# Delta-net stage of a two-layer trunk: background modulation held back during the block inverses, its weights in other buffers, longer planned inverse steps

## The chip, the cores and the metric

The kernel runs on one core of one Trainium2 chip. The metric is the device time of one execution in microseconds (us), as the median of several runs. One execution was also recorded by the hardware profiler; durations and starts below come from that one.

A core has five engines that run side by side, each with an instruction queue of its own that is worked off in order: TensorE (PE in the profile; PEld is its weight load), VectorE (DVE), ScalarE (ACT), GpSimd (POOL) and SyncE (SP), which here only starts transfers. A `q` behind an engine's name is its sequencer, which issues DMAs and waits on semaphores.

## The reference

A trunk of two layers on x of shape 1024 x 1024 (float32). Each layer is a mixer, a layer norm, a convolutional feed-forward and a layer norm; layer 0 mixes with a gated delta net, layer 1 with retention. Every layer is modulated by a condition vector:

```
e = silu(c @ cond_w + cond_b)
for i in range(2):
    mod = e @ ada_w[i] + ada_b[i]
    sh1, sc1, g1, sh2, sc2, g2 = split(mod, 6)
    y = mixers[i](x * (1 + sc1) + sh1)
    x = layer_norm(alpha * x + (1 + g1) * y)
    y = conv_ffn(x * (1 + sc2) + sh2)
    x = layer_norm(alpha * x + (1 + g2) * y)
```

The delta net, which the change touches, has 8 heads of width 128 and chunks of 64 positions:

```
q, k, v = split(silu(causal_dwconv((h @ w_in)[qkv])))
kk  = strict_lower(kb @ k.T * decay)
sol = triangular_solve(kk + eye, [v * beta, kb * exp(gc)])      # u, w
scan over chunks:  v_new = u - w @ state
                   o = (q * exp(g)) @ state + qk @ v_new
                   state = state * exp(g_last) + (k * exp(g_last - g)).T @ v_new
o = rmsnorm(o) * norm_w * silu(z);  return o @ w_out
```

The vectors of `mod` that later steps of layer 0 need (sc2, sh2, g1) are computed inside the delta-net stage, as "background modulation".

## The kernel before, in words

**Filler.** The big matmuls of the stage are those of `h @ w_in`: a unit makes 128 output features for all 1024 positions, as two halves of 8 x 3 matmuls of 128x128 by 128x512 (each product is made of three, because the operands are split into a high and a low part). There are three leftover halves ("h"), 21 units for q, k and v ("c" items) and eight gate units ("z" items). `filler` (L1028 to L1071) runs them in the order of `items` (L1080); a "c" item takes two of the 24 `qkv` buffers, and when fewer than two are free and more than four gate units are left, a gate unit is taken in its place (L1032). A unit's weights come by one 512 KB transfer into the two-buffer tag `wr` (L102), are split by ACT (L89) and DVE (L90, `wl`), and each half of a "c" unit costs DVE three convolution steps (L435).

**Background modulation.** `bg_ada` queues eight units for each of three vectors (24 in all, L1017 to L1019). A unit loads 256 rows of `ada_w` (512 KB, tile `mvw`, L210), in the tag `bg_tag[0]`, which is `wr` here, and DVE adds the two 128-row blocks, weighted by `e`, onto the one `ada` tile (L214, L216). Every fourth unit is followed by four transposes on PE (L226) and four ACT sums (L228). `filler` calls `bg_step` once after every "c" and "z" item (L1071).

**Block inverse.** The triangular solve goes by an explicit inverse. `t_solve` (L766) inverts the 32x32 diagonal blocks of four heads at once, on DVE: `X` is gathered by ACT (L773), transposed (L777), and then 31 steps of a multiply (L785) and a subtract (L787) run one after the other; at every second step the function yields `LAT["fs"]` (L788). Then come a transpose (L791), a copy on ACT (L793) and another transpose (L795). There are two such solves, for heads 0 to 3 and 4 to 7.

**The rest of the heads' work.** `t_front` makes the matrices U (L719 to L764), `t_chain` joins the 32-blocks to 64-blocks with small matmuls on PE (L807 to L888), `prep` and `dt_half` make scaled v, k and q-k products (L897, L898, L932, L933, with `DT` loaded at L925 into a `lane` or `auh` buffer), and `scan` runs the 8 chunk steps of each head (L940), with a `tail` per half head (L988).

**What sets the order.** `run` (L627) is a planner in the Python that builds the program: it keeps a clock `clk` that every PE instruction advances by a planned cost (0.216 us for a 512-wide matmul), and of the streams whose time has come it always goes on with the one of the lowest priority number; a stream that yields a number sleeps for that much planned time. The filler has priority 9.0, a solve 0.3 and 2.3. PE's order is fixed by this plan (`pq`, L607). The other engines' orders are not pinned: the framework orders each of them from the instructions' dependencies and a timeline of its own, in which an instruction that comes later in the program can go ahead when it is ready; buffers of a tag are handed out in program order.

Of the kernel before, what the change touches and what calls it, by code (L numbers as in the profile page):

```python
# [12 lines left out]
ALU = mybir.AluOpType  # L13
AX = mybir.AxisListType

P = 128
D = 1024
S = 1024
KT = D // P
HALF = 512  # L20
# [13 lines left out]
def trunk_kernel(ctx: ExitStack, tc, A):  # L34
    nc = tc.nc
    pe, act, dve, pool, sp = nc.tensor, nc.scalar, nc.vector, nc.gpsimd, nc.sync
# [9 lines left out]
    def tl(tag, shape, dt=F32, name=None):  # L46
        return sb.tile(shape, dt, tag=tag, name=name or tag, bufs=BUFS[tag])
# [66 lines left out]
    bg = []  # L114

    bg_ps = [None]
    bg_tag = ["wr"]

    def bg_step(tile=mm_tile):
        bg_ps[0] = tile  # L120
        if bg:
            bg.pop(0)()
# [58 lines left out]
    e = ct("e", [P, KT])  # L181
# [19 lines left out]
    def bg_ada(i, j, kind):  # L201
        box = {}

        def unit(nh, kp):
            if kp == 0:
                box["a"] = tl("ada", [P, HALF])
            a = box["a"]
            wr = tl(bg_tag[0], [P, 2, HALF], name="mvw")
            c0 = j * D + nh * HALF
            sp.dma_start(wr, A["ada_w"][i, kp * 256:(kp + 1) * 256, c0:c0 + HALF].rearrange("(a p) n -> p a n", p=P))  # L210
            for kk in range(2):
                k = kp * 2 + kk
                if k == 0:
                    dve.tensor_scalar(a, wr[:, 0], e[:, 0:1], None, ALU.mult)  # L214
                else:
                    dve.scalar_tensor_tensor(a, wr[:, kk], e[:, k:k + 1], a, ALU.mult, ALU.add)  # L216
            if kp < KT // 2 - 1:
                return
            if kind == "col":
                if nh == 0:  # L220
                    vecs[i, j] = ct(f"v{i}{j}", [P, KT])
                gs = slice(4 * nh, 4 * nh + 4)
                v, b = vecs[i, j][:, gs], bias_cols(i, j)[:, gs]
                tp, pt = bg_ps[0](), tl("sm2", [P, 4], name="cs")
                for g in range(4):
                    pe.transpose(tp[:, g * P:(g + 1) * P], a[:, g * P:(g + 1) * P], ident)  # L226
                for g in range(4):
                    act.activation(a[:, g * P:(g + 1) * P], tp[:, g * P:(g + 1) * P], AF.Copy, accum_out=pt[:, g:g + 1])  # L228
                if j in (1, 2, 4):
                    dve.scalar_tensor_tensor(v, pt, 1.0, b, ALU.add, ALU.add)  # L230
                else:
                    dve.tensor_add(v, pt, b)
            else:
                if nh == 0:
                    rows[i, j] = row_load(A["ada_b"][i:i + 1, j * D:(j + 1) * D], ("x", i))
                g = rows[i, j][nh]
                pt = bg_ps[0]()
                pe.matmul(pt, ones, a, start=True, stop=True)
                dve.scalar_tensor_tensor(g, pt, 1.0, g, ALU.add, ALU.add)

        for nh in range(2):
            for kp in range(KT // 2):
                bg.append(lambda nh=nh, kp=kp: unit(nh, kp))
# [196 lines left out]
    ssq = {}  # L440
# [61 lines left out]
    xT = {}  # L502
# [121 lines left out]
    def emit(name, lat=0.0):  # L624
        events[name] = clk[0] + lat
# [45 lines left out]
    def take(tag, n):  # L671
        while free[tag] < n:
            yield lambda: free[tag] >= n
        free[tag] -= n

    def give(tag, n):
        free[tag] += n
# [6 lines left out]
    def gates():  # L684
# [18 lines left out]
        dve.tensor_sub(gl64, g64, gh64)  # L703
        emit(("g",), LAT["g1"])
        yield LAT["g1"]
        pt = mm_tile()
# [9 lines left out]
    def decay(h):  # L716
        for q4 in range(2):
            yield from take("t2", 2)
            gm = [tl("t2", [P, 4, P], F32R, name="gm") for _ in range(2)]  # L719
            for t, g in zip(gm, (gh64, gl64)):  # L720
                pool.tensor_tensor(t, bm(m_incl, 4), bc(g[:, q4s(q4), h], P), ALU.mult)
            yield LAT["gm"]
            pt = mm_tile()
# [5 lines left out]
    def t_front(p):  # L729
# [8 lines left out]
        for h in pairs[p]:  # L738
# [4 lines left out]
            for q4 in range(2):  # L743
                yield LAT["kk"]
                pt = mm_tile()
# [20 lines left out]
    def t_solve(qd_):  # L766
        yield after_ev(("T0", 2 * qd_ - 1), ("A", 2 * qd_), ("A", 2 * qd_ + 1))
        yield from take("lane", 1)
        X = tl("lane", [P, 32, 32], name="X")
        for h in pairs[2 * qd_] + pairs[2 * qd_ + 1]:  # L770
            for b in range(4):
                bs = slice(32 * b, 32 * b + 32)
                act.activation(X[bs, :, h % 4 * 8:h % 4 * 8 + 8].rearrange("p i c -> p c i"), U[h][bs, :, bs], AF.Copy)  # L773
        yield from take("lane", 2)
        yield LAT["X"]
        Y = tl("lane", [P, 32, 32], name="Y")
        dve.transpose(flat(Y), flat(X))  # L777
        T = tl("lane", [P, 32, 32], name="T")
        pool.memset(T, 0.0)
        pool.memset(flat(T)[:, 0:1024:33], 1.0)  # L780
        tmp = tl("fs", [P, 256], name="fs")
        for j in range(31):
            ni, nj = 31 - j, j + 1
            tv = tmp[:, 0:ni * nj].rearrange("p (i j) -> p i j", j=nj)
            dve.tensor_tensor(tv, bc(Y[:, j + 1:, j], nj), bm(T[:, j, 0:nj], ni), ALU.mult)  # L785
            ts_ = T[:, j + 1:, 0:nj]
            dve.tensor_tensor(ts_, ts_, tv, ALU.subtract)  # L787
            if j % 2:  # L788
                yield LAT["fs"]
        RX = tl("lane", [P, 32, 32], name="RX")  # L790
        dve.transpose(flat(RX), flat(T))  # L791
        TP = tl("lane", [P, 32, 32], name="TP")
        act.activation(TP, T.rearrange("p i j -> p j i"), AF.Copy)  # L793
        TX = tl("lane", [P, 32, 32], name="TX")
        dve.transpose(flat(TX), flat(TP))  # L795
        RTX[qd_] = (RX, TX)
        give("lane", 1)
        emit(("Tq", qd_))
        emit(("T", qd_), LAT["T"])

# [187 lines left out]
    def tail(p, h, q4):  # L988
# [3 lines left out]
        act.activation(d, o, AF.Square)  # L992
        dve.tensor_reduce(so, d, AX.X, ALU.add)
        dve.scalar_tensor_tensor(so, so, 1.0 / P, ssq[h][:, qs], ALU.mult, ALU.add)
# [28 lines left out]
    def ssq_late(ti):  # L1023
        yield LAT["ssq"]
        ssq_tile(ti, ptr)
        emit(("f", ti), 1.0)

    def filler(items):  # L1028
        spare = [(z, k) for k in range(GH)]
        todo = list(items)  # L1030
        while todo or spare:
            if not todo or (todo[0][0] == "c" and free["qkv"] < 2 and len(spare) > 4):  # L1032
                kind, ti = spare.pop(0)
            else:
                kind, ti = todo.pop(0)
            if kind == "h":
                if ti > 1:
                    acc = acc_tile()
                    for k in range(KT):
                        mm3(acc, ws[ti], k, hT[1][k], k == 0, k == KT - 1, pm)  # L1040
                        yield 0.0
                    first_out(ti, 1, acc)
                if first[ti] < GH:
                    yield [(0.2, ssq_late(first[ti]))]
                else:
                    emit(("f", first[ti]), LAT["fv"])
                continue
            w = load_w(A["gdn_wqkv" if kind == "c" else "gdn_wz"][ti])
            prev = None
            if kind == "c":  # L1050
                feats[ti] = []
            for half in range(2):
                if kind == "c":
                    yield from take("qkv", 1)
                acc = acc_tile()
                for k in range(KT):
                    mm3(acc, w, k, hT[half][k], k == 0, k == KT - 1, pm)
                    yield 0.0
                if kind == "c":
                    feats[ti].append(tl("qkv", [P, HALF], name="qkv"))  # L1060
                    prev = conv_half(ti, acc, half, feats[ti], prev)
                else:
                    cv = tl("cv", [P, 516], name="sg")
                    act.activation(cv[:, 0:HALF], acc, AF.Silu)  # L1064
                    act.dma_start(zd[ti, :, hs(half)], cv[:, 0:HALF])
            if kind == "c":
                if ti < GH:
                    yield [(0.2, ssq_late(ti))]
                else:
                    emit(("f", ti), LAT["fv"])  # L1070
            bg_step(acc_tile)  # L1071

    LAT = {"kk": 3.05, "ld": 1.14, "g1": 17.30, "gm": 2.50, "mm": 1.81, "T": 4.98, "X": 3.38, "fs": 1.9, "T0": 5.00, "t1": 1.65, "t2": 2.35, "t3": 1.34, "D": 2.67, "s1": 1.60, "s2": 1.22, "s3": 1.26, "tail": 12.31, "ssq": 9.30, "fv": 2.85}
    pairs = [(2 * p, 2 * p + 1) for p in range(GH // 2)]
    for nm in ("S", "T0", "Dt", "M", "Tq"):
        events[nm, -1] = 0.0
# [55 lines left out]
    def strassen(hT0, xts, scale, shift, items, tags=("hTb", "hTb", "qkv", "qkv", "aux"), direct=False, beside=None):  # L1132
# [7 lines left out]
        def side(n, s):  # L1140
            out = []
            for u in items[n][:2]:
                w = load_w(u)
                X = acc_tile()
                for i, b in enumerate((("11", "21"), ("12", "22"))[s]):
# [414 lines left out]
    g1 = two("auh", F32, "g1")  # L1560
# [373 lines left out]
```

## Time and profile before

| what | value |
|---|---|
| median of 3 runs | 2995.94 us (2995.53 to 2998.75) |
| the profiled execution | 2992.3 us |
| span of its trace | 2990.3 us |
| granted TensorE clock, mean | 0.98 |
| delta-net stage with the filler, about 100 to 656 us | some 556 us of the span |

The span is the part of the execution that the trace covers; the profiled execution lies 2.0 us above its span and 3.6 us below the median. A row of the timeline reads: start, duration, engine, line, operation, output and inputs, shape, count, and in brackets the engine's idle time before it and what released it. A row of a table by windows reads: the window, its length, then busy time and instruction count of each engine, the granted clock, the DMA engines' mean busy share, and GB/s. A row of a waits list reads: who waited, for whom, total us, how often, the longest.

### The profile page before, as it was taken

To read this page: it belongs to the slowest core of one execution; us is meant where nothing else is said; L and a number is where in the kernel's file an instruction comes from. 1 tells how busy PE (TensorE), PEld (TensorE's weight loads), DVE (VectorE), ACT (ScalarE), POOL (GpSimd) and SP (SyncE) were. 2 spreads that over 40 slices of the span, in tenths; PEclk is the share of its full clock that TensorE was granted. 3 is DMA by queue.
4 is the path that set the end of the run, shared out by engine and by line. 5 is a ranking of instruction groups with operands and counts; after the bars stand their busy time and mean duration, and the time that the engine had idled before them with its cause. 6 is when DMAs were issued, how large, how long until landed. Compare 5 with 4: busy or idle time off the path is not lost.

```text
span 2990.3 us, 38893 instructions
## 1 busy us (share of the span) xinstructions
PE 2827.8 (95%) x13638; PEld 2308.4 (77%) x13638; DVE 2191.9 (73%) x3877; ACT 1347.4 (45%) x2513; POOL 604.6 (20%) x629
## 2 busy tenths in 40 slices
PE   8889998999999999999999989989999899999996
PEld 7768877887778888877787777767778688888785
DVE  5785687545588888997677665656687787778888
ACT  4655555434544444536443333212345544445444
POOL 0411221133011111520002330232201011112603
PEclk9999999999999999999999999999999999999998
DMA  7222221344344444864424453556573333335652
GB/s 273 86 77 72 96 89 64 117 159 137 110 141 162 155 151 147 311 204 135 154 79 145 157 210 119 170 169 183 169 248 125 127 134 106 106 106 200 242 179 106
DMA packets 235379, 442.35 MB, mean 148 GB/s; under 512 B 22192, under 2 KB 75696, under 8 KB 235184
## 3 DMA queue, kind: packets, MB, share of 16 engines
q1 hardware_dynamic: 205024, 387.96, 38.9%
q10 hardware_dynamic: 25152, 34.61, 3.2%
q0 software_dynamic: 5008, 17.30, 1.5%
q8 instruction: 107, 1.75, 0.2%
q14 instruction: 88, 0.72, 0.1%
HBM read 331.26 MB, written 108.53 MB: 147 GB/s over the span
## 4 chain that ended last, share of the span: by engine, by line
PE 68%; DVE 13%; issue 8%; DMA 6%; ACT 4%; POOL 2%; SPq 0%; POOLq 0%; ACTq 0%; DVEq 0%
PE acc L616 15%; PE acc L1412 11%; PE acc L1138 8%; PE acc L110 5%; PE acc L111 4%; PE acc L112 4%; PE sc L616 4%; PE sc L1138 3%; PE sc L1412 3%; PE mm L616 2%; PE sc L111 2%; PE sc L110 2%; PE sc L112 2%; DMA mvw<-in_ada_w 1%; DVE qkv L435 1%
## 5 line engine op out<-in xcount | busy, mean ns | idle before, releaser
L1412 PE MATMUL acc<-bb,ab 128*128 128x512 f32 x1800 | 427.7, 392 | 3.7 <-DVE bb L90 1.5
L1412 PEld LDWEIGHTS acc<-bb,ab 128*128 128x128 f32 x1800 | 337.3, 188 | 78.2 <-DVE bb L90 3.9
L616 PE MATMUL acc<-hT,wh 128*128 128x512 f32 x960 | 301.2, 395 | 0.0
L1548 POOL TENSOR_TENSOR o<-o 128x512 f32<-128x512 f32 x88 | 118.3, 1354 | 719.5 <-DVE o L1541 684.7
L1138 PE MATMUL acc<-T,wb 128*128 128x512 f32 x840 | 209.4, 400 | 12.6 <-DVE wb L90 12.6
L616 PEld LDWEIGHTS acc<-hT,wh 128*128 128x128 f32 x960 | 183.4, 191 | 33.8
L616 PE MATMUL acc<-hT,wl 128*128 128x512 f32 x480 | 203.5, 424 | 0.2 <-ACT sg L1064 0.2
L89 ACT ACTIVATE ab<-ar 128x512 fp32r<-128x512 f32 x210 | 129.4, 624 | 158.7 <-PE acc L1412 85.6
L1138 PEld LDWEIGHTS acc<-T,wb 128*128 128x128 f32 x840 | 161.2, 193 | 50.6 <-DVE wb L90 16.9
L90 DVE TENSOR_TENSOR ab<-ar,ab 128x512 fp32r<-128x512 f32 x210 | 172.9, 830 | 30.1 <-ACT ab L89 29.7
L90 DVE TENSOR_TENSOR wb<-wr,wb 128x512 fp32r<-128x512 f32 x162 | 114.2, 710 | 86.8 <-ACT wb L89 86.5
L90 DVE TENSOR_TENSOR wl<-wr,wh 128x1024 fp32r<-128x1024 f32 x85 | 104.2, 1225 | 97.3 <-ACT wh L89 97.3
L89 ACT ACTIVATE wh<-wr 128x1024 fp32r<-128x1024 f32 x101 | 106.8, 1058 | 129.9 <-PE acc L616 61.5
L90 DVE TENSOR_TENSOR wb<-mm,wb 128x512 fp32r<-128x512 f32 x216 | 145.1, 685 | 21.1 <-ACT wb L89 19.1
L1197 ACT ACTIVATE pc<-acc 128x512 f32<-128x512 f32 x143 | 84.6, 592 | 160.9 <-PE acc L1138 108.2
L89 ACT ACTIVATE wb<-mm 128x512 fp32r<-128x512 f32 x216 | 122.4, 593 | 76.5 <-DVE mm L1184 76.2
L89 ACT ACTIVATE wb<-wr 128x512 fp32r<-128x512 f32 x162 | 98.9, 626 | 98.8 <-DMA wr<-in_ffn_up 49.5
L616 PE MATMUL acc<-wh,hT 128*128 128x512 f32 x384 | 137.1, 420 | 2.5 <-DVE vv L90 1.6
L1527 DVE SCALAR_TENSOR_TENSOR o<-g,vc,o 128x512 f32<-128x512 f32 (+2 forms) x176 | 135.3, 787 | 0.9 <-ACT o L1522 0.2
L435 DVE SCALAR_TENSOR_TENSOR qkv<-raw,vc,qkv 128x512 f32<-128x512 f32 x144 | 114.8, 801 | 26.8 <-ACT qkv L433 25.5
L216 DVE SCALAR_TENSOR_TENSOR ada<-mvw,e,ada 128x512 f32<-128x512 f32 x140 | 107.1, 765 | 27.2 <-DMA mvw<-in_ada_w 27.1
L110 PE MATMUL acc<-T,wb 128*128 128x512 f32 x292 | 116.7, 400 | 9.9 <-DVE wb L90 9.4
(620 smaller groups left out, 7079.8 us busy)
## 6 DMA issues: line engine op xcount, KB each, us to landing
wr<-in_ffn_up SPq DMA_DIRECT2D x96, 512.0 KB, 4.4
mvw<-in_ada_w SPq DMA_DIRECT2D x80, 512.0 KB, 4.4
ad<-o SPq DMA_DIRECT2D x154, 256.0 KB, 2.3
ar<-ad SPq DMA_DIRECT2D x154, 256.0 KB, 4.0
Br<-in_ffn_down SPq DMA_DIRECT2D x66, 256.0 KB, 3.8
wr<-in_ret_wv SPq DMA_DIRECT2D x32, 512.0 KB, 3.9
ar<-od SPq DMA_DIRECT2D x56, 256.0 KB, 5.2
xs<-xt ACTq DMA_DIRECT2D x24, 512.0 KB, 3.1
```

Of the source, the lines that this page charges most:

```text
L89: act.activation(dst_h, src, AF.Copy)
L90: eng.tensor_tensor(dst_l, src, dst_h, ALU.subtract)
L110: mm(acc, wl[:, k], hl[0], start=first, stop=False)
L111: mm(acc, wh[:, k], hl[1], start=False, stop=False)
L112: mm(acc, wh[:, k], hl[0], start=False, stop=last)
L216: dve.scalar_tensor_tensor(a, wr[:, kk], e[:, k:k + 1], a, ALU.mult, ALU.add)
L435: dve.scalar_tensor_tensor(oh, raw[:, 3 - j:515 - j], w[:, 3 - j:4 - j], oh, ALU.mult, ALU.add)
L616: pq(pe.matmul(out, lhsT, rhs, start=start, stop=stop, **kw), cost)
L1138: return pe.matmul(*a, skip_group_check=True, **kw)
L1412: mm_ = (lambda *a, p=p, onto=onto, **kw: (mm if p < 2 else pe.matmul)(*a, skip_group_check=onto, **kw))
L1527: dve.scalar_tensor_tensor(tv, gv[:, c0 - j:c1 - j], w[:, 2 - j:3 - j], tv, ALU.mult, ALU.add)
L1548: pool.tensor_tensor(o[d], o[x], o[y], op)
```

## The change

The tag of the background weights in the delta-net stage becomes `xT` (two buffers of 128x512, used earlier in the kernel for two of the transposed inputs), so that a unit issues two 256 KB transfers in place of one of 512 KB, and `wr` is left to the filler's weights. A list `busy` is filled when a solve starts and emptied when it ends. `filler` counts an owed step after each item; while a solve is busy it makes none, otherwise up to two. `LAT["fs"]` goes from 1.9 to 2.2. The tag is set to `lane` and then `wr` by the feed-forward of layer 0, as before, so that later stages load as they did.

```diff
-    bg_tag = ["wr"]
+    bg_tag = ["xT"]
...
-            wr = tl(bg_tag[0], [P, 2, HALF], name="mvw")
             c0 = j * D + nh * HALF
-            sp.dma_start(wr, A["ada_w"][i, kp * 256:(kp + 1) * 256, c0:c0 + HALF].rearrange("(a p) n -> p a n", p=P))
+            src = A["ada_w"][i, kp * 256:(kp + 1) * 256, c0:c0 + HALF].rearrange("(a p) n -> p a n", p=P)
+            if bg_tag[0] == "xT":
+                wr = [tl("xT", [P, HALF], name="mvw") for _ in range(2)]
+                for a2 in range(2):
+                    sp.dma_start(wr[a2], src[:, a2])
+            else:
+                wt = tl(bg_tag[0], [P, 2, HALF], name="mvw")
+                sp.dma_start(wt, src)
+                wr = [wt[:, 0], wt[:, 1]]
...
-                    dve.scalar_tensor_tensor(a, wr[:, kk], e[:, k:k + 1], a, ALU.mult, ALU.add)
+                    dve.scalar_tensor_tensor(a, wr[kk], e[:, k:k + 1], a, ALU.mult, ALU.add)
...
     def t_solve(qd_):
         yield after_ev(("T0", 2 * qd_ - 1), ("A", 2 * qd_), ("A", 2 * qd_ + 1))
         yield from take("lane", 1)
+        busy.append(qd_)
...
         give("lane", 1)
+        busy.clear()
         emit(("Tq", qd_))
...
+    busy, owed = [], [0]
+
     def filler(items):
...
-            bg_step(acc_tile)
-
-    LAT = {"kk": 3.05, "ld": 1.14, "g1": 17.30, "gm": 2.50, "mm": 1.81, "T": 4.98, "X": 3.38, "fs": 1.9, "T0": 5.00, "t1": 1.65, "t2": 2.35, "t3": 1.34, "D": 2.67, "s1": 1.60, "s2": 1.22, "s3": 1.26, "tail": 12.31, "ssq": 9.30, "fv": 2.85}
+            owed[0] += 1
+            for _ in range(0 if busy else min(owed[0], 2)):
+                bg_step(acc_tile)
+                owed[0] -= 1
+
+    LAT = {"kk": 3.05, "ld": 1.14, "g1": 17.30, "gm": 2.50, "mm": 1.81, "T": 4.98, "X": 3.38, "fs": 2.2, "T0": 5.00, "t1": 1.65, "t2": 2.35, "t3": 1.34, "D": 2.67, "s1": 1.60, "s2": 1.22, "s3": 1.26, "tail": 12.31, "ssq": 9.30, "fv": 2.85}
```

2 lines of the change are left out of this document (1 added, 1 removed).

## The prediction

> **What bounds the kernel now.** I read the page first, then the delta-net stage by windows, then the waits of PE in it, and last the timelines of PE and DVE around the two block inverses.
>
> ```profile
> span 2990.3 us, 38893 instructions
> PE 2827.8 (95%) x13638; PEld 2308.4 (77%) x13638; DVE 2191.9 (73%) x3877; ACT 1347.4 (45%) x2513; POOL 604.6 (20%) x629
> ```
>
> PE is busy for 95% of the span, so what can be won lies in the gaps of PE. The windows (length, then busy time of PE, PEld, DVE, ACT, POOL, the granted clock, DMA share, GB/s) show where the stage has them.
>
> ```profile
> 100.00:660.00 560.00, 511.68 (x3470) 434.19 (x3469) 388.46 (x948) 296.44 (x650) 117.49 (x164) 0.97 0.27 92
> 172.00:218.10 46.10, 37.32 (x188) 30.54 (x186) 42.64 (x97) 18.19 (x55) 1.39 (x6) 0.98 0.23 76
> 203.00:224.00 21.00, 6.80 (x42) 5.07 (x41) 17.62 (x40) 6.58 (x12) 4.20 (x11) 0.82 0.14 50
> 453.00:475.00 22.00, 10.12 (x64) 8.42 (x63) 20.33 (x47) 11.36 (x39) 4.74 (x11) 0.86 0.23 75
> 490.00:630.00 140.00, 134.87 (x993) 117.17 (x992) 76.65 (x177) 64.52 (x165) 16.17 (x23) 0.98 0.33 115
> ```
>
> PE stands still for 560.00 - 511.68 = 48.3 us of the stage, and 14.2 (21.00 - 6.80) and 11.9 (22.00 - 10.12) of it lie at the ends of the two solves: 26.1 us. The waits of PE name the reason:
>
> ```profile
> PE mm L616 <- DVE DT L933: 19.8, 2, 11.0
> PE mm L619 <- DVE DT L933: 2.5, 2, 1.7
> PE mm L616 <- DVE qkv L898: 3.5, 3, 1.4
> ```
>
> ```profile
> 202.13 1.04 PE L619 MATMUL mm<-cst,qkv 128*128 128x128 f32 x8
> 211.36 1.16 PE L616 MATMUL mm<-qkv 128*128 128x128 f32 x8
> 223.52 2.08 PE L616 MATMUL mm<-qkv 128*128 128x128 f32 x8 [11.00 <-DVE DT L933]
> ```
>
> ```profile
> 171.92 1.25 DVE L777 STREAM_TRANSPOSE Y<-X 128x1024 f32<-128x1024 f32 x1 [0.45 <-ACT X L773]
> 177.65 0.75 DVE L216 SCALAR_TENSOR_TENSOR ada<-mvw,e,ada 128x512 f32<-128x512 f32 x1 [1.22 <-DMA mvw<-in_ada_w]
> 187.12 0.75 DVE L216 SCALAR_TENSOR_TENSOR ada<-mvw,e,ada 128x512 f32<-128x512 f32 x1 [0.77 <-DMA mvw<-in_ada_w]
> 217.94 1.25 DVE L791 STREAM_TRANSPOSE RX<-T 128x1024 f32<-128x1024 f32 x1
> 222.78 1.50 DVE L933 TENSOR_TENSOR DT<-DT,mm 128x512 f32<-128x512 f32 x2 [1.59 <-DMA DT<-Ld]
> ```
>
> The plan puts the first work after the solve (the transposes of `prep`) at 202.13 in PE's order, but DVE ends the inverse only at 217.9. The last buffer of `lane` comes free with the copy behind it, DT is loaded into that, its product (L933) runs at 222.78, and PE, whose order is pinned, has had nothing else since 212.52 (211.36 + 1.16). In the second solve the same wait lasts 8.82 us. DVE is the limit here (42.64 us busy of the 46.10 from 172 to 218.1), PE everywhere else in the stage. The gate units, the filler's last, still run after the scans:
>
> ```profile
> 628.54 14.58 PE acc L616 x65
> 643.56 12.29 PE acc L616 x54
> ```
>
> So 26.9 us of filler (these two pieces of the chain) are in hand at the end, and filler that PE does inside a solve shortens the stage one for one.
>
> **The change part by part.** *More issue time.* In plan time a triple of filler matmuls costs 3 x 0.216 = 0.648, and a solve goes on at the first triple after its sleep: 1.9 is three triples (1.944), 2.2 is four (2.592). So each of the 15 yields of a solve lets through one triple more, 45 matmuls in all.
>
> ```profile
> 200.08 0.39 PE L616 MATMUL acc<-hT,wl 128*128 128x512 f32 x1
> 200.76 0.39 PE L616 MATMUL acc<-hT,wl 128*128 128x512 f32 x1
> ```
>
> A triple takes 0.68 us of PE, so PE arrives 15 x 0.68 = 10.2 us later at the end of each solve. Where scores and transposes of other streams fall into the sleep it may be less: from below 15 x 0.3 = 4.5 us.
>
> *No modulation in the solves.* DVE's modulation adds (L216) in the windows of the two inverses:
>
> ```profile
> 172.00:218.10 46.10, 3.70 (x5) 0.98 0.23 76
> 420.00:469.10 49.10, 5.97 (x8) 1.00 0.28 88
> ```
>
> First solve: 3.70, and the 1.22 and 0.77 that DVE stood for the weights, are 5.7 us removed. Second: 5.97 and one short multiply of 0.48 (below), 6.4.
>
> ```profile
> 465.65 0.48 DVE L214 TENSOR_SCALAR ada<-mvw,e 128x512 f32<-128x512 f32 x1
> 473.73 0.69 DVE L933 TENSOR_TENSOR DT<-DT,mm 128x512 f32<-128x512 f32 x1
> 474.47 2.08 PE L616 MATMUL mm<-qkv 128*128 128x128 f32 x8 [8.82 <-DVE DT L933]
> ```
>
> Against this the 45 matmuls more are 45/48 of a unit, whose DVE work falls into the same solve: six convolution steps of 0.67 us from start to start and a split of 1.13, 5.2 x 45/48 = 4.8 us. These come from
>
> ```profile
> 183.51 0.75 DVE L435 SCALAR_TENSOR_TENSOR qkv<-raw,vc,qkv 128x512 f32<-128x512 f32 x1
> 184.18 0.34 DVE L785 TENSOR_TENSOR fs<-Y,T 128x175 f32<-128x175 f32 x1
> 203.01 1.22 DVE L90 TENSOR_TENSOR wl<-wr,wh 128x1024 fp32r<-128x1024 f32 x1
> 204.14 0.42 DVE L785 TENSOR_TENSOR fs<-Y,T 128x252 f32<-128x252 f32 x1
> ```
>
> First solve: DVE ends 5.7 - 4.8 = 0.9 us earlier, so PE may go on at 223.52 - 0.9 = 222.6. It arrives at 212.52 + 10.2 = 222.7, less whatever goes of the small waits before it, which the list gives as 3.5 us for L898 and 2.5 for L619 in both solves, some 3 us in each. Between 0 and 3 us are left of 14.2; I take 3, a gain of 11. Second solve: 6.4 - 4.8 = 1.6 earlier, 472.9; PE arrives at 474.47 - 8.82 + 10.2 = 475.9, less about 3 of small waits. Taken as 1 us left of 11.9: a gain of 11.
>
> *The clock.* After the 11.00 us wait the eight matmuls took 2.08 us, before it 1.16; over both solves I count 2 us (from 0 to 4).
> The Trainium skill, "TensorE: Matmul & The Clock Gate", Part 1, says that an idle window of some 3.4 us halves the clock and that it takes about as long of work to get it back; by that rule a wait that shrinks below 3.4 us gives back up to 1.7 us a solve, an estimate from the page, and one of 5 us nothing. The 2.08 agrees with half speed.
>
> *The made-up steps.* A unit is 16 triples, 10.9 us of PE, so in each solve, 46 us and more, about four units end, so eight steps come as second ones behind a first. Their DVE work, 2 x 0.67 us, moves into 240 to 300 and after 490, where DVE is busy for 76.65 of 140 us. What it can cost is DVE standing for the transfer with the scans' short operations queued behind.
>
> ```profile
>   DMA mvw<-in_ada_w: 13.8, 12
> DMA to landing us min/median/max: 3.7/3.8/4.4
> ```
>
> Now DVE stands 13.8 us in 12 such places, 1.2 us a time, and the list of PE's waits has no entry that names L216. A second step's transfer can start only when the first step's adds have freed `xT`; SP waits there too, with `wr` loads and DT loads behind it. Between 0 (hidden by PE's planned slack) and 8 x (3.8 + 1.3) = 41 us (the whole landing, all of it seen by PE); I take 5 us, near the 1.2 a time of the row, since PE's own waits put it close to the lower end. Below nothing isn't excluded: the buffers of their own let a single step's weights be loaded before they are wanted, and the filler's weights no longer wait for them. I leave that at 0; the 13.8 bound it.
>
> *Two transfers for one.*
>
> ```profile
> 68.58 0.38 SPq L210 DMA_DIRECT2D mvw<-in_ada_w  x1
> mvw<-in_ada_w SPq DMA_DIRECT2D x21, 512.0 KB, 3.8
> DT<-Ld SPq DMA_DIRECT2D x16, 256.0 KB, 2.7
> ```
>
> The 24 more issues hold SP for at most 0.38 us each, 9 us in some 500: hidden. Half the size lands in 2.7 and not in 1.9 us, so two in a row cost a little more than one.
> The Trainium skill, "DMA: Bandwidth & Descriptors", Rules for kernel authors, speaks against it: small transfers should be joined into one large one, each carrying a fixed 2 us by its anatomy section. By it the 24 would cost up to 48 us of transfer time, an estimate; the DMA engines' share of 0.27 says that it is hidden.
>
> *The stage's end.* 26.9 - 2 x 10.2 = 6.5 us of filler are left behind the scans, so no hole opens there by the plan, but the last gate products and the next stage's loads stand closer together; 2 us off.
>
> Sum: 11 + 11 + 2 - 5 - 2 = 17 us. The profiled execution took 2992.3, of which 2990.3 is span and 2.0 lies around it, so it should become 2975.3. The median lies 3.6 above it: 2995.94 - 17 = 2979.
>
> **The rivals.** *First: the modulation stays in the solves.* Only PE's order is pinned.
>
> ```profile
> 111.61 0.58 ACT L430 ACTIVATE raw<-acc 128x512 f32<-128x512 f32 x1
> ```
>
> The first step's transfer, which the program writes behind a unit that ends at 111.6, started at 68.58 (above). So a step written after the solve may be drawn into it again, and with buffers of its own all the more. Then only the issue time works: the first solve ends 4.8 later, PE goes on at 228.3 and arrives at about 219.7 to 222.7: 6 to 8 us left, 7 won; the second at 479.3 against 475.9, 4 left, 8 won, and no doubles to pay. With 3 us of disorder: 12 won, 2984. Against it: the steps now rank behind convolutions and inverse, and `ada` has one buffer.
>
> *Second: the scans bound the end.* If they stay where they are, the last tail still ends at 644.3 and the next stage can't be drawn far ahead of it:
>
> ```profile
> 643.60 0.69 ACT L1008 ACTIVATE ot<-mm,vc 128x512 f32<-128x512 f32 x1 [3.93 <-PE mm L619]
> 655.68 1.05 PE L1566 MATMUL mm<-dg,ones 128*128 128x128 f32 x8
> ```
>
> Then at most 655.7 - 644.3 = 11 are won, less 3 of disorder: 8, 2988. For it: the scans follow the solves, which end hardly earlier in time. Against it: the next stage's first half needs only the first half of the last head.
>
> *Third, slower: the second steps stall DVE beside the scans.* The price is the 41 us above, against 24 won: 17 slower, 3013. It decides from 24 / 8 = 3.0 us of PE time a step. Against it stand the 1.2 us a stall that the trace shows and the 63 us (140.00 - 76.65) for which DVE has nothing to do in the last scans' window.
>
> **How the numbers follow.** The forecast has a chance of 0.58, the first rival 0.18, the second 0.12, the third 0.12. A measurement of this kernel can tell about 0.2%, 6 us, from no change. Of the forecast nearly all is faster by more; of the first rival 0.15, of the second 0.07; the rest of these and 0.03 of the third make "same"; 0.09 is slower. That is 0.79, 0.12 and 0.09. The range goes down to 26.1 + 4 = 30 us won (2966), and up to the second rival and its disorder, 3 us won (2993); the third rival is left out.
>
> **What would show it.** The 11.00 and 8.82 us waits for L933 should fall below 3 us each; L216 and L214 should have no more than one operation inside either inverse (rival one: five and nine, as now); between two pairs of inverse steps PE should run four triples; the mean clock from 218 to 240 should rise above 0.81. PE waits that name u, Sn or w beside the modulation steps would show the third rival, and idle PE after the last scan the second. The forecast is wrong if PE's idle time in the stage stays above 40 us.

## The result and the profile after

| | before | after |
|---|---|---|
| median | 2995.94 us | 2977.53 us |
| lowest and highest of 7 runs each | 2987.61 to 2998.75 | 2968.14 to 2986.36 |
| span of the profiled execution | 2990.3 us | 2975.8 us |

The ratio after to before is 0.9942, 95% interval 0.9923 to 0.9962: faster by 17 us (11 to 23). In a second measurement, told below, the same kernel had 0.9964 (0.9949 to 0.9979), 11 us. The forecast was 2979 with a range of 2966 to 2993.

A time of the whole kernel says little about one stage here, so the stage is read from the trace. Before, the first matmul of the output projection (L315) starts at 656.49 us; after, the same one (L322 there) starts at 645.38: the stage is 11.1 us shorter. The remaining 3.4 us of the difference between the spans lie behind it. What lies behind the stage is written the same in all the kernels of this study, and it took between 2327.0 us (2954.1 - 627.06) and 2340.3 us (2997.6 - 657.31) in their traces. So the times carry up to 13 us that the stage didn't make. The stage's length moves with the clock too: in the run with holding back alone (below), whose clock was low, 9.7 of 12.5 us more were PE's busy time. So PE's idle time in the stage, length less busy time, stands beside the ratios below. It isn't exact either, for each trace is one execution.

The windows of the kernel after (columns as before: window, length, PE, PEld, DVE, ACT, POOL, clock, DMA share, GB/s): the stage, both inverses from the first transpose to the last (L785, L799), and the two stretches around their ends.

```profile
100.00:645.38 545.38, 507.44 (x3463) 430.33 (x3461) 382.04 (x936) 294.19 (x649) 119.00 (x165) 0.98 0.26 91
170.90:221.42 50.52, 47.30 (x233) 38.91 (x232) 47.31 (x103) 22.58 (x61) 0.98 (x7) 1.00 0.24 80
427.72:474.59 46.87, 46.23 (x222) 38.54 (x221) 43.13 (x96) 22.78 (x62) 1.03 (x8) 1.00 0.13 47
203.00:227.10 24.10, 15.32 (x85) 12.26 (x83) 20.62 (x46) 10.66 (x18) 4.06 (x11) 0.94 0.18 66
455.00:482.00 27.00, 23.23 (x122) 19.49 (x122) 21.95 (x47) 18.35 (x57) 5.56 (x16) 0.97 0.17 59
```

PE's idle time in the stage fell from 48.3 to 37.9 us (545.38 - 507.44). At the solves' ends it fell from 14.2 to 8.8 (24.10 - 15.32) and from 11.9 to 3.8 (27.00 - 23.23), 13.5 us together; elsewhere it rose by 3.1. The first inverse has 233 matmuls beside it where the one before had 188 between the same two transposes: 45 more, the one triple a yield of the prediction. The second has 222 for 213; of the filler alone, which reads `hT`, it has 186 for 157, 29 more. These are its filler matmuls, before and after:

```profile
420.00:469.10 49.10, 36.65 (x157) 28.83 (x155) 0.00 (x0) 0.00 (x0) 0.00 (x0) 1.00 0.28 88
427.72:474.59 46.87, 42.99 (x186) 34.34 (x185) 0.00 (x0) 0.00 (x0) 0.00 (x0) 1.00 0.13 47
```

The waits of PE in the stage, and the rows of PE and DVE at the solves' ends, of the kernel after:

```profile
PE mm L623 <- DVE DT L942: 8.2, 2, 5.6
PE mm L626 <- DVE DT L942: 1.6, 2, 0.8
PE mm L623 <- DVE qkv L907: 1.9, 2, 1.5
PE acc L322 <- DVE hl L90: 2.9, 1, 2.9
```

```profile
211.30 1.04 PE L626 MATMUL mm<-cst,qkv 128*128 128x128 f32 x8
227.03 2.08 PE L623 MATMUL mm<-qkv 128*128 128x128 f32 x8 [5.55 <-DVE DT L942]
480.24 1.95 PE L623 MATMUL mm<-qkv 128*128 128x128 f32 x8 [2.62 <-DVE DT L942]
```

```profile
174.30 0.75 DVE L223 SCALAR_TENSOR_TENSOR ada<-mvw,e,ada 128x512 f32<-128x512 f32 x1 [0.74 <-DMA mvw<-in_ada_w]
177.94 0.75 DVE L223 SCALAR_TENSOR_TENSOR ada<-mvw,e,ada 128x512 f32<-128x512 f32 x1 [0.58 <-DMA mvw<-in_ada_w]
179.48 0.75 DVE L223 SCALAR_TENSOR_TENSOR ada<-mvw,e,ada 128x512 f32<-128x512 f32 x1 [0.37 <-DMA mvw<-in_ada_w]
221.42 1.25 DVE L799 STREAM_TRANSPOSE RX<-T 128x1024 f32<-128x1024 f32 x1
226.29 1.45 DVE L942 TENSOR_TENSOR DT<-DT,mm 128x512 f32<-128x512 f32 x2 [1.63 <-DMA DT<-Ld]
```

The work behind the first solve now stands at 211.30 in PE's order and not at 202.13. But the modulation adds (L223) still run in that inverse, and DVE stands for their weights. The windows of the adds alone, first and second inverse, and their transfers on SP:

```profile
170.90:221.42 50.52, 3.71 (x5) 1.00 0.24 80
427.72:474.59 46.87, 0.00 (x0) 1.00 0.13 47
```

```profile
48.34 1.01 SPq L213 DMA_DIRECT2D mvw<-in_ada_w  x2
62.44 11.52 SPq L213 DMA_DIRECT2D mvw<-in_ada_w  x6
169.81 10.78 SPq L213 DMA_DIRECT2D mvw<-in_ada_w  x6
399.67 13.11 SPq L213 DMA_DIRECT2D mvw<-in_ada_w  x7
```

The steps run in blocks of four, each as soon as the one `ada` tile is free: 48 to 73, 164 to 181, 268 to 283, 329 to 346, 400 to 416, 520 to 530. The second block is written behind the first solve, and was drawn into it. Of the fifth, three steps of four are written behind the second solve; they were drawn ahead too, and happened to end before its inverse began, which so has no add at all. Which steps are written where shows in the run with the order enforced (below), where the weights of these steps are loaded only behind the two solves (the two at 394.99 are the fifth block's first step):

```profile
217.59 14.35 SPq L213 DMA_DIRECT2D mvw<-in_ada_w  x8
394.99 2.65 SPq L213 DMA_DIRECT2D mvw<-in_ada_w  x2
473.39 12.12 SPq L213 DMA_DIRECT2D mvw<-in_ada_w  x6
```

### The profile page after: what moved, and what is told of

It reads as the page before. It is cut to its first block, busy times and chain, and to the rows that moved or that the text cites. A ratio compares the mean times of both kernels' runs of the same rounds, so it can differ in the third digit from the quotient of the medians.

```text
span 2975.8 us, 38952 instructions
## 1 busy us (share of the span) xinstructions
PE 2820.7 (95%) x13638; PEld 2300.1 (77%) x13638; DVE 2191.7 (74%) x3877; ACT 1347.4 (45%) x2513; POOL 606.4 (20%) x629
## 4 chain that ended last, share of the span: by engine, by line
PE 67%; DVE 12%; issue 8%; DMA 7%; ACT 4%; POOL 2%; SPq 0%; POOLq 0%; DVEq 0%; ACTq 0%
PE acc L623 14%; PE acc L1426 11%; PE acc L1152 8%; PE acc L110 5%; PE acc L111 4%; PE acc L112 4%; PE sc L1152 4%; PE sc L623 4%; PE mm L623 2%; PE sc L1426 2%; DMA mvw<-in_ada_w 2%; PE sc L110 2%; PE sc L111 2%; PE sc L112 2%; PE mm L626 1%
## 5 line engine op out<-in xcount | busy, mean ns | idle before, releaser
L623 PE MATMUL acc<-hT,wh 128*128 128x512 f32 x960 | 299.3, 393 | 0.0
L623 PEld LDWEIGHTS acc<-hT,wh 128*128 128x128 f32 x960 | 182.3, 190 | 34.0
L623 PE MATMUL acc<-hT,wl 128*128 128x512 f32 x480 | 202.2, 421 | 0.6 <-ACT ada L235 0.4
L90 DVE TENSOR_TENSOR ab<-ar,ab 128x512 fp32r<-128x512 f32 x210 | 167.1, 802 | 28.0 <-ACT ab L89 27.7
L90 DVE TENSOR_TENSOR wb<-wr,wb 128x512 fp32r<-128x512 f32 x162 | 114.5, 711 | 93.3 <-ACT wb L89 91.4
L90 DVE TENSOR_TENSOR wl<-wr,wh 128x1024 fp32r<-128x1024 f32 x85 | 105.6, 1243 | 93.1 <-ACT wh L89 91.0
L90 DVE TENSOR_TENSOR wb<-mm,wb 128x512 fp32r<-128x512 f32 x216 | 145.0, 684 | 22.1 <-ACT wb L89 20.1
L623 PE MATMUL acc<-wh,hT 128*128 128x512 f32 x384 | 137.0, 419 | 2.7 <-DVE vv L90 1.6
L223 DVE SCALAR_TENSOR_TENSOR ada<-mvw,e,ada 128x512 f32<-128x512 f32 x140 | 107.1, 765 | 32.3 <-DMA mvw<-in_ada_w 32.1
```

Source lines behind the costliest of these rows:

```text
L90: eng.tensor_tensor(dst_l, src, dst_h, ALU.subtract)
L223: dve.scalar_tensor_tensor(a, wr[kk], e[:, k:k + 1], a, ALU.mult, ALU.add)
L623: pq(pe.matmul(out, lhsT, rhs, start=start, stop=stop, **kw), cost)
```

## The experiments

Four theories stood against each other. Before the change PE idles 48.3 us in the stage. A: the longer issue time carries the gain, by giving PE cover. B: DVE freed of modulation carries it. C: the buffers of their own carry it. D, formed after the first four runs: issue time and holding back work only together.

**Issue time alone.** In the kernel before, one figure of the line `LAT`:

```diff
-"fs": 1.9
+"fs": 2.2
```

> Only the issue time of the inverse steps is changed, 1.9 to 2.2. Theory A (the issue time carries the gain, since PE gets one filler triple more per yield): about 10 us faster, the idle time of PE at the two solve ends together falls from 26.1 to some 14 us, with as many modulation adds inside the inverses as before. Theory B (DVE freed of modulation carries it): at most 4 us faster. Theory C (the buffers of their own carry it, by earlier weights): no difference.

Ratio 0.9997 (0.9984 to 1.001): nothing. PE's idle time is 45.6 us (557.31 - 511.76), 2.8 less. The window of this kernel's first inverse:

```profile
173.44:228.82 55.38, 50.61 (x237) 41.65 (x235) 50.96 (x112) 23.59 (x69) 1.30 (x7) 0.91 0.29 92
```

The same window for the adds alone:

```profile
173.44:228.82 55.38, 7.43 (x10) 0.91 0.29 92
```

And PE's wait for DT in the stage (sum in us, times, longest):

```profile
PE mm L616 <- DVE DT L933: 16.5, 2, 9.8
```

Theory A falls as the whole cause. PE got its triples (237 matmuls), but the first inverse took 55.38 us in place of 46.02, with ten adds (7.43 us) where five (3.70) were. Our reading is that with more filler in the solve the unit that releases the next block of four ends inside it, and the block runs there too. The two waits one by one:

```profile
234.49 2.08 PE L616 MATMUL mm<-qkv 128*128 128x128 f32 x8 [6.68 <-DVE DT L933]
494.02 2.08 PE L616 MATMUL mm<-qkv 128*128 128x128 f32 x8 [9.84 <-DVE DT L933]
```

Counted from the start of the first inverse, PE came to the wait 13.8 us later than before (54.37 us, which is 234.49 - 6.68 - 173.44, against 212.52 - 171.92 = 40.60) and its work 9.4 us later (61.05 against 51.60), so 4.3 of the 11.00 us went. But 45 matmuls more are only 10.2 us; the rest of PE's delay is its own slowness, at a granted clock of 0.91 in this inverse (0.98 before). With 10.2 us of cover against 9.4 of delay some 10 us of the wait would be left, an estimate. At the second solve the wait didn't shrink (9.84 against 8.82). What idle time lost, busy time gained: PE was busy 3.6 us longer in the stage (511.76 against 508.17), at a granted clock of 0.95 against 0.97.

**Issue time 1.95.** The same, smaller, in the kernel before:

```diff
-"fs": 1.9
+"fs": 1.95
```

> Only the issue time is changed, 1.9 to 1.95. If a solve goes on at the first filler triple after its sleep (three triples are 1.944 of plan time, four are 2.592), 1.95 gives four triples a yield as 2.2 does, and the kernel is the same as with 2.2 alone within 3 us. If the plan follows the number itself, 15 x 0.05 us a solve are 1.5 us in all and nothing is seen.

Ratio 0.9993 (0.9981 to 1.0006); the first inverse took 55.61 us with the same 237 matmuls and ten adds. So the plan does round up to whole triples: 0.05 does what 0.3 does. PE's idle time is 42.4 us (559.33 - 516.98), 6.0 less than before and 3.2 less than with 2.2, with 8.8 us more busy time than before: so 3 us of idle time between two profiles, here of much the same plan, say little.

**Holding back alone.** In the changed kernel:

```diff
-    bg_tag = ["xT"]
+    bg_tag = ["wr"]
...
-"fs": 2.2
+"fs": 1.9
```

> Only the holding back of modulation steps while a solve is planned, with the weights in the old buffers and the old issue time. Theory A: the first inverse still holds about five modulation adds, because the engines' orders are not pinned and the steps are drawn ahead; the second holds none to four; 0 to 5 us faster. Theory B: no adds inside either inverse and 10 us or more faster. Theory C: no difference.

Ratio 1.0033 (1.0019 to 1.0046), 10 us slower by twelve executions, which no theory had. Seven adds run in each inverse (5.22 and 5.24 us; before five and eight), so nothing was held back on DVE. The stage is 12.5 us longer, 2.8 of it idle time of PE and 9.7 its busy time, with the same work. The windows of the stage and of two stretches in it, in the row order of the text:

```profile
100.00:668.97 568.97, 517.91 (x3455) 438.75 (x3454) 388.63 (x944) 295.03 (x649) 114.24 (x163) 0.95 0.27 90
420.00:490.00 70.00, 56.60 (x329) 46.76 (x329) 53.13 (x112) 35.15 (x85) 7.36 (x24) 0.88 0.21 68
490.00:560.00 70.00, 65.41 (x598) 55.40 (x591) 43.37 (x97) 32.97 (x84) 5.90 (x15) 0.90 0.20 62
```

The granted clock was 0.88 and 0.90 there, against 0.93 and 0.95 in the kernel before. The waits at the solves' ends (19.8 us for DT, as before) are not what makes this kernel slower. The clock is in part: over all executions on this chip its mean was 0.9765 (median of 12) against 0.978 (median of 35 of the kernel before). Taken as time at half clock that is some 9 us, which costs PE half, 4.5 of the 10 us, an estimate. The rest stays open.

**Buffers alone.** In the changed kernel:

```diff
-        busy.append(qd_)
...
-        busy.clear()
...
-            owed[0] += 1
-            for _ in range(0 if busy else min(owed[0], 2)):
-                bg_step(acc_tile)
-                owed[0] -= 1
+            bg_step(acc_tile)
...
-"fs": 2.2
+"fs": 1.9
```

> Only the buffers of the modulation weights are changed (two transfers of half the size into xT), no holding back, old issue time. Theories A and B: within 4 us of before; the modulation steps run earlier, in blocks of four as soon as the accumulator tile is free. Theory C: 8 us or more faster, with DVE standing less for weights.

Ratio 0.9999 (0.9987 to 1.0012): theory C falls as a cause of its own, and PE's idle time rose to 55.6 us (564.02 - 508.39). The second inverse took 56.96 us with fourteen adds (10.50 us): with buffers of their own two blocks were drawn into it. PE waited 29.9 us for DT, 19.0 at one place.

**Issue time and holding back**, old buffers. In the changed kernel:

```diff
-    bg_tag = ["xT"]
+    bg_tag = ["wr"]
```

> Issue time 2.2 and holding back, with the weights in the old buffers. Theory D (interplay: the longer issue time alone lets one more unit end inside the solve and so draws a further block of four modulation steps into the inverse, and the holding back keeps that block out): 10 to 18 us faster than before, as the changed kernel, five to seven adds in the first inverse and not ten. Theory C (own buffers are needed as well): within 6 us of before.

Ratio 0.9967 (0.9954 to 0.9981): 10 us. The first inverse has seven adds and took 52.77 us, not 55.38; the second has six adds, where the issue time alone has eight. The two waits:

```profile
228.11 2.08 PE L623 MATMUL mm<-qkv 128*128 128x128 f32 x8 [5.98 <-DVE DT L942]
489.88 2.08 PE L623 MATMUL mm<-qkv 128*128 128x128 f32 x8 [5.20 <-DVE DT L942]
```

So holding back takes 0.7 us off the first wait (6.68 with the issue time alone, at a lower clock) and 4.6 off the second (9.84), although theory D had named the first. The profiled execution was the slowest of eight (2992.43 us against a median of 2986.65), and its stage ends at 656.06, as before the change: PE's idle time is 41.7 us (556.06 - 514.35), 6.6 less, while its busy time for the same work is 6.2 more. This is theory D by the times, by the waits for DT (11.2 us in sum, against 16.5 and 19.8 with either part alone) and by the idle time, which falls by more than the two parts give alone (-2.8, or -6.0 with 1.95, and +2.7), but not by the stage's length.

**Issue time and buffers**, no holding back. In the changed kernel, the same lines as for the buffers alone, with `fs` left at 2.2:

```diff
-        busy.append(qd_)
...
-        busy.clear()
...
-            owed[0] += 1
-            for _ in range(0 if busy else min(owed[0], 2)):
-                bg_step(acc_tile)
-                owed[0] -= 1
+            bg_step(acc_tile)
```

> Issue time 2.2 and buffers of their own, without holding back. Theory D: no faster than before (within 5 us), ten or more adds in an inverse. Theory C: most of the gain, 10 us or more.

Ratio 0.999 (0.9981 to 1.0): at most 6 us. PE's idle time is 44.8 us (553.67 - 508.88), 3.5 less. The adds in this kernel's first inverse:

```profile
172.00:229.93 57.93, 8.94 (x12) 0.96 0.32 102
```

There are twelve, more than with either part alone, and PE's wait for DT is nearly as long as with the issue time alone:

```profile
PE mm L623 <- DVE DT L940: 15.3, 2, 10.7
```

**The order enforced.** In the changed kernel:

```diff
-                if k == 0:
-                    dve.tensor_scalar(a, wr[0], e[:, 0:1], None, ALU.mult)
-                else:
-                    dve.scalar_tensor_tensor(a, wr[kk], e[:, k:k + 1], a, ALU.mult, ALU.add)
+                with after("solve"):
+                    if k == 0:
+                        dve.tensor_scalar(a, wr[0], e[:, 0:1], None, ALU.mult)
+                    else:
+                        dve.scalar_tensor_tensor(a, wr[kk], e[:, k:k + 1], a, ALU.mult, ALU.add)
...
-        dve.transpose(flat(TX), flat(TP))
+        anchor["solve"] = dve.transpose(flat(TX), flat(TP))
...
+    anchor.pop("solve")
```

> The changed kernel, and the modulation adds of steps that the program makes after a solve are ordered on DVE behind that solve's last transpose, so that none can be drawn ahead into it. Theory D: no adds in the first inverse, which ends some 4 us earlier; the wait of 5.55 us for DT there shrinks to 1 to 2 us; 3 to 6 us faster than the changed kernel, if the blocks behind the solve cost nothing. If adds beside the scans are dear (the third rival of the prediction), it is slower than the changed kernel.

Ratio 0.9948 (0.9932 to 0.9964). By the times it can't be told from the changed kernel. By the trace the holding back is real now: no add in either inverse, the first takes 47.24 us (50.52), the longest wait for DT is 2.4 us (5.55), and the projection starts at 639.74, 5.6 us earlier than in the changed kernel. But 4.4 of these 5.6 us were there when the first inverse began (166.51 against 170.90), and PE's idle time from 100 us on is 35.6 us, 2.3 less than in the changed kernel. So the adds kept out of the inverse are worth less than the start of the projection says. The adds alone in the window of the first inverse:

```profile
166.51:213.75 47.24, 0.00 (x0) 1.00 0.16 55
```

And all engines in the window of the stage:

```profile
100.00:639.74 539.74, 504.12 (x3453) 428.08 (x3451) 380.54 (x934) 293.35 (x647) 117.48 (x163) 0.98 0.27 92
```

**No modulation in the stage**, the three vectors set to one:

```diff
-    bg_ada(0, 4, "col")
-    bg_ada(0, 3, "col")
-    bg_ada(0, 2, "col")
+    for j in (4, 3, 2):
+        vecs[0, j] = ct(f"v0{j}", [P, KT])
+        pool.memset(vecs[0, j], 1.0)
```

> The changed kernel without the 24 modulation steps of the stage: the three vectors are set to one, nothing is loaded or added for them. A bound on what modulation costs the stage at all. Theory D: the first solve's wait falls as in the run with the enforced order, and 8 to 14 us are won against the changed kernel, half of it at the start and beside the scans. If modulation is hidden everywhere but in the solves: 3 to 6 us.

Ratio 0.9882 (0.9867 to 0.9897), 35 us. The projection starts at 627.06, 18.3 us earlier than in the changed kernel, more than expected. 10.4 us of that is idle time of PE, the rest its busy time. The profiled execution was the fastest of four. So the modulation is not hidden in this stage, and moving it can win only a part of what it costs; with this plan of PE's work, this is the bound for any order of it.

**Holding back and buffers.** In the changed kernel:

```diff
-"fs": 2.2
+"fs": 1.9
```

> The changed kernel with the old issue time of 1.9. Theory D (the parts work only together): no faster than before by more than 4 us, and possibly slower by up to 10 as with the holding back alone; the waits for DT at the two solve ends stay near 20 us. If holding back and the buffers carry the gain by themselves: 10 us or more faster.

Ratio 0.9992 (0.9979 to 1.0004): no gain, as theory D has it; PE's idle time is 48.3 us (559.49 - 511.21), as before. Against holding back alone (1.0033) the buffers do win here, some 12 us by the times, with intervals that lie apart. PE's waits for DT in this kernel:

```profile
PE mm L623 <- DVE DT L942: 22.0, 2, 11.0
```

**Issue time 2.65**, five triples, in the changed kernel:

```diff
-"fs": 2.2
+"fs": 2.65
```

> The changed kernel with an issue time of 2.65, which is five filler triples a yield and not four. If PE were still short of cover at the solve ends, the 8.2 us of waits for DT vanish and it is 3 to 6 us faster than the changed kernel. If DVE is the bound by now (more filler brings its own convolutions into the inverse, 4.8 us for 10.2 us of PE) or the filler runs out behind the scans (the second rival of the prediction): no faster, or up to 10 us slower.

Ratio 0.9989 (0.9976 to 1.0001). The profiled execution was the fastest of twelve (2984.64 us against a median of 2993.75). Near the ends of the two solves PE has work, and the idle time is back at other places. The windows around the solves' ends, two others, and the stage's end:

```profile
207.09:229.09 22.00, 17.72 (x97) 15.01 (x96) 19.73 (x42) 14.12 (x36) 5.38 (x11) 0.99 0.16 50
464.76:486.76 22.00, 22.00 (x103) 18.23 (x102) 18.26 (x37) 14.30 (x37) 5.70 (x14) 1.00 0.22 73
360.00:420.00 60.00, 49.26 (x255) 40.45 (x255) 45.78 (x140) 34.36 (x60) 16.87 (x22) 0.94 0.28 93
490.00:560.00 70.00, 61.03 (x511) 51.30 (x512) 39.13 (x77) 33.98 (x95) 3.54 (x11) 0.93 0.22 72
630.00:643.81 13.81, 7.88 (x56) 6.59 (x55) 8.79 (x24) 8.15 (x17) 5.75 (x4) 0.93 0.49 169
```

4.3 us of idle time are left at the first solve's end and none in the window of the second. But PE idles 10.7 us from 360 to 420 and 9.0 from 490 to 560, against 6.5 and 5.6 in the changed kernel, and 6.37 us of the 9.0 are one wait for `qkv` right behind the second solve:

```profile
495.66 2.07 PE L623 MATMUL mm<-qkv 128*128 128x128 f32 x8 [6.37 <-DVE qkv L907]
```

And the filler runs out: its last matmuls start at 629.60 (641.44 in the changed kernel), PE idles 5.9 us from there to the projection (13.81 - 7.88), and the last copies of the tails run 9 us later than in the changed kernel, whose row is the second:

```profile
655.79 1.25 ACT L1017 ACTIVATE ot<-mm,vc 128x512 f32<-128x512 f32 x2
646.78 0.68 ACT L1017 ACTIVATE ot<-mm,vc 128x512 f32<-128x512 f32 x1
```

The projection starts at 643.81, 1.6 us earlier than in the changed kernel, but here that isn't the end of the stage. PE's idle time is 39.2 us (543.81 - 504.64). This is the second case of the expectation: no faster, with the filler spent too early.

**The order enforced at the start too**: the adds of the first four steps behind the first convolutions. In the kernel with the order enforced:

```diff
-            dve.scalar_tensor_tensor(oh, raw[:, 3 - j:515 - j], w[:, 3 - j:4 - j], oh, ALU.mult, ALU.add)
+            anchor["cv"] = dve.scalar_tensor_tensor(oh, raw[:, 3 - j:515 - j], w[:, 3 - j:4 - j], oh, ALU.mult, ALU.add)
...
+    anchor["solve"] = anchor["cv"]
```

> The run with the enforced order, and in addition the adds of the first four steps ordered behind the first convolutions, so that they leave the loading of x (48 to 73 us) alone. The first filler drain should come some 5 us earlier, as before the change. If that carries through: 2 to 5 us faster than with the enforced order alone, 2974 to 2978 us. If the early block only trades places with DVE work before the first solve: no difference.

Ratio 0.9972 (0.996 to 0.9983), not better. The first drain of the filler came at 75.63, as before the change (75.54; after it 80.43). But PE was busy for only 30.44 us of 100 to 140, against 35.89 with the early block, and the stage ended 10.5 us later than with the order enforced behind the solves alone, 4.6 of it idle time of PE (40.2 against 35.6). That the block, moved behind the convolutions, takes DVE time that is scarcer there is our reading of these windows, and no run tests it alone.

**The changed kernel again.**

> The changed kernel once more, beside the others on the same chip: 2977 us within its own spread of about 9 us, first wait for DT 5 to 6 us, five modulation adds in the first inverse and none in the second.

Median 2985.53 us, ratio 0.9964 (0.9949 to 0.9979); the projection starts at 645.84, the waits for DT are 8.2 us, five adds in the first inverse and none in the second. PE's idle time is 38.0 us (545.84 - 507.83), against 37.9 in the first profile: this repeats, the time of the whole does not. The profiled execution (2975.36 us) was the second fastest of the twelve, so the stage as read here is that of a quick execution.

**The runs side by side.** The waits are those of the eight matmuls (L616, later L623) for DT behind the two solves; the adds leave out the multiply that begins a block.

| kernel | ratio | adds in 1st, 2nd inverse | wait behind 1st, 2nd solve, us | PE idle, us | projection starts |
|---|---|---|---|---|---|
| before | 1 | 5, 8 | 11.00, 8.82 | 48.3 | 656.49 |
| issue time 2.2 | 0.9997 | 10, 8 | 6.68, 9.84 | 45.6 | 657.31 |
| issue time 1.95 | 0.9993 | 10, 8 | 6.79, 9.41 | 42.4 | 659.33 |
| holding back | 1.0033 | 7, 7 | 11.08, 8.67 | 51.1 | 668.97 |
| buffers | 0.9999 | 5, 14 | 10.94, 18.97 | 55.6 | 664.02 |
| issue time, holding back | 0.9967 | 7, 6 | 5.98, 5.20 | 41.7 | 656.06 |
| issue time, buffers | 0.999 | 12, 7 | 10.71, 4.61 | 44.8 | 653.67 |
| holding back, buffers | 0.9992 | 5, 7 | 10.99, 10.98 | 48.3 | 659.49 |
| all three (the change) | 0.9942 | 5, 0 | 5.55, 2.62 | 37.9 | 645.38 |
| the same again | 0.9964 | 5, 0 | 5.69, 2.56 | 38.0 | 645.84 |
| all three, order enforced | 0.9948 | 0, 0 | none, 2.44 | 35.6 | 639.74 |

## Why the prediction was right

The first measurement came out where the forecast was, 17 us, and with the kind of gain that it named: PE stands less at both solves' ends. But that the number fits is in part luck. The stage itself is 11.1 us shorter, the second measurement gave 11 us, and both lie nearer to the first rival's 12 us than to the forecast. Both gains of 11 us were mis-sized, each by another step.

*First solve: DVE was not freed.* Counted from the start of the inverse, PE came to the wait after 50.58 us (227.03 - 5.55 - 170.90) where it was 40.60 (212.52 - 171.92) before: 10.0 us later, as the 10.2 of the forecast. But its work was ready after 56.13 us where it was 51.60: 4.5 us later, where 0.9 earlier was forecast. The step "5.7 us removed" failed: five adds (3.71 us) and 1.7 us of standing for weights are still in this inverse, and DVE ended it at 221.42, where 217.0 was worked out and 222.7 by the first rival. So the first rival, that the steps are drawn back, holds here: 8.8 us of idle time are left, and 5.4 were won.

*Second solve: less cover, and a free inverse by luck.* PE came after 49.90 us (480.24 - 2.62 - 427.72) where it was 45.54 (474.47 - 8.82 - 420.11): 4.4 us later and not 10.2, with 29 more filler matmuls in the inverse and not 45. Its work was ready 1.8 us earlier (1.6 worked out), with an inverse free of adds. It is free because its block ran ahead of the solve, not because the steps stayed behind it. 8.1 us were won of the 11.

*The signs.* The waits for DT are 5.55 and 2.62 us, where both were to fall below 3; the inverses hold five adds and none, where one at most was forecast; the mean clock from 218 to 240 is 0.84, above 0.81 as forecast; PE's idle time is 37.9 us, below the 40 from which the forecast was to be called wrong.

*The clock* was to give 2 us; PE's busy time in the stage fell by 0.7. Eight matmuls took 2.08 us after the first wait, as before, and 1.95 after the second, of 2.62 us. The granted clock right behind that second wait:

```profile
480.20:482.00 1.80, 1.76 (x9) 1.76 (x10) 0.69 (x1) 1.74 (x5) 1.47 (x5) 0.56 0.00 0
482.00:484.00 2.00, 2.00 (x9) 1.76 (x8) 1.38 (x2) 1.95 (x4) 0.00 (x0) 0.54 0.00 0
```

The Trainium skill, "TensorE: Matmul & The Clock Gate", Part 1, ties the drop to half clock to an idle window of some 3.4 us. Here the measurement decides: a wait of 2.62 us, with waits of 0.78 and 0.37 us in the 7 us before it, was enough.

*The made-up steps and the stage's end* were to cost 5 and 2 us. Idle time away from the solves' ends rose by 3.1 us, and 2.88 of that is one new wait: PE stands before the projection for DVE's `hl` (L90), where before the change it was busy without a gap from 600 to 655 us. So the stage's end costs the 3.1 nearly alone, and the made-up steps cost nothing that shows. The third rival is out: DVE stood 17.8 us in 21 places for modulation weights, 0.8 a time, and PE's waits for `Sn`, `w` and `u` of the scans are 4.8 us against 5.1 before. The second rival did not come as worked out, for the projection started 1.4 us ahead of the last tail's copy (646.78). But its sign, idle PE behind the filler, is there with these 2.88 us: the filler's reserve is used up, and a larger issue time gains nothing.

*Two transfers for one* were to be hidden, and nothing in the runs speaks against it: the buffers alone gave 0.9999, and 256 KB landed in 3.0 us (median) where 512 KB took 3.8. The anatomy section of "DMA: Bandwidth & Descriptors" in the Trainium skill, from which the prediction has its fixed 2 us, is about transfers that GpSimd issues. These are issued by SP, and no term of the sum rests on the figure.

The stage's sum is then 13.5 + 0.7 - 3.1 = 11.1 us, where 17 was forecast.

What the prediction didn't see is that the terms don't add. By the times the issue time alone wins nothing, holding back alone nothing or less, and both together 10 us. The waits show where. With the old issue time the first wait stays at 11 us and the second near 9 us or above, whatever else is changed. With the new one the first falls to 5.5 to 6.8 us, except where twelve adds run in the inverse (10.71). The second stays at 9.84 with the issue time alone and falls to 5.20 with holding back, to 4.61 with the buffers and to 2.62 with both. At the first solve the adds give the reason: cover for PE also brings a block of modulation into the same inverse (ten and twelve adds for five), and holding back keeps that block out rather than emptying the inverse. That ten adds left only 6.68 us goes with the clock of 0.91 there. At the second the issue time alone adds none (eight, as before). Counted from the start of that inverse PE comes only 2.6 us later (48.14 us against 45.54) and its work 3.6 us later (57.98 against 54.36); why PE gets so little there isn't shown. Whether the buffers add to the other two parts stays open: the ratio of 0.9967 without them lies inside the interval of the second measurement with them. PE's idle time is 3.7 us less with them (41.7 against 38.0 and 37.9), but that rests on one profile without, of the slowest of eight executions, and two with.

## What to carry to other kernels

Where only one engine's order is pinned, moving a step in the program doesn't move it on the others: count the operations in the window that they were to leave, and order them behind an instruction of their own engine if they must stay out. Cover for a waiting engine is worth little if the cover itself brings work to the engine that is waited for; work out both ends of the wait. Where the whole moves by its own spread, read a change from the trace, stage by stage: but look where the profiled execution lies among all, and whether the old stage's last work is really done when the next one starts.

## What the runs showed of the hardware

The granted clock falls in stretches where PE is hardly idle. In the run with holding back alone it was 0.90 from 490 to 560, with PE busy for 65.41 of 70 us, and inside that at half for some 10 us with PE busy throughout:

```profile
500.00:505.00 5.00, 5.00 (x37) 4.14 (x35) 0.75 (x2) 3.20 (x6) 0.00 (x0) 0.50 0.15 42
505.00:510.00 5.00, 5.00 (x17) 4.01 (x16) 1.44 (x3) 1.28 (x2) 0.23 (x2) 0.52 0.20 66
```

The longest wait in the 10 us before was 1.35 us. PE's busy time in the stage, from 100 us to the projection, was between 504.1 and 517.9 us in the runs that had all of its work: 13.8 us apart, as much as the whole gain. Behind the stage, where the programs agree, the spans differ by up to 13 us.
